# The SSD output projection as seven block products, the first norm's transposes later, and another split of the last output projection of cross attention

## The chip, the cores and the metric

The kernel runs on one core of one Trainium2 chip. The metric is device time in microseconds (us), the median of three runs. Engines: TensorE (PE) multiplies, VectorE (DVE) and ScalarE (ACT) work element by element, GpSimd (POOL) does a little of the same, SyncE (SP) issues most transfers.

## The reference

One post-norm decoder layer on 512 tokens of width 1024, everything in fp32. The kernel must give the layer's output for all 512 tokens.

```python
proj = x @ w_in                              # z, x|B|C, dt and q, k, v, gate
y_ssd = gated_rms_norm(ssd_scan(silu(conv(xbc)), dt) , silu(z))
y_ret = swish_gate(group_norm(retention(rotary(q), rotary(k), v)), g)
mix = concat(y_ssd, y_ret) @ w_out           # (512, 2048) @ (2048, 1024)
x = LN(ALPHA * x + mix)
k, v = mem @ w_xk, mem @ w_xv                # 256 memory tokens
x = LN(ALPHA * x + (softmax(x @ w_xq @ k.T * scale) @ v) @ w_xo)   # 4 heads of 256
x = LN(ALPHA * x + ffn(x))                   # up 1024 -> 2 x 2752, conv of 3, SiLU gate, down
```

## The kernel before

Every fp32 product is made of three fp32r matmuls (`mm3`): high part by high part, high by low, low by high. High parts are casts, low parts what the cast left. A weight group is 128 x 1024: `Group.split` loads it into one of three raw slots (L141, SyncE's queue), casts it on ScalarE (L143), and subtracts on VectorE (L144), or on GpSimd if the group was planned with `pool=True`. High and low part lie in a ring of four pairs `wh`, `wl`. `Stream` hands the groups out in the order of `plan`, loading ahead.

The 512 tokens are four tiles of 128 (`t` = 0 to 3). A product by tokens (`tok`) gives a PSUM bank of 128 tokens x 512 outputs, a product by features (`feat`) a bank of 128 features x tokens. Activations are split in the same way when they leave PSUM: ScalarE casts (L260), VectorE subtracts (L261).

For some projections the work is done in blocks: `Quarters` holds a weight as four quarters in two halves each and makes sums of quarters (L184 to L191); `Sides` does the same with the activations (splits L351 and L352, sums L372 to L375). Seven products of half the size in every direction, in the order 11, 21, T2, T1, T3, 22, T4, then replace eight; each is added into the accumulator `acc[t]` as it comes (L893, or L895 with the scale ALPHA). Their weight parts are made at L196 and L197. `SEVEN` lists the projections done so: the value projection `v` and the FFN's `down`. Between the products of `down`, groups of the up projection stand by the table `UP_MIX`.

TensorE's instructions are pinned in the order in which the program writes them; the other engines' order is set by a scheduler at build time from the dependencies. Each engine takes its queue strictly in order.

The stages that the change touches, in the order of the program:

- *Retention's output projection*, then the *SSD output projection*: eight weight groups, 24 matmuls of 128x512 each, for all four token tiles, and four additions at the end of each half (L893).
- *First norm*, beside the *memory keys*: `norm` takes the variance (L952, L953), a reciprocal root on GpSimd (L464, L465) and two scalings of 128x1024 (L957, L964). `norm_t` transposes the normed tile (eight transposes, L112). The keys are 8 features in 4 heads, 32 steps of six 128x256 matmuls; then 16 steps of the memory values. The low parts of the keys' eight weight groups are made on GpSimd. `first_norm` says after how many steps each tile's transposes come.
- *Cross attention*, four heads: `x_head(h)` weaves scores, softmax (maximum L1073, exponent L1076, reciprocal L1078, scaling L1080), transposes of the probabilities and values into dense work, which is the next head's query, and for the last head a part of the output projection `w_xo`.
- *Second norm*: `last` adds the rest of `w_xo` token by token (L1138), and each token is normed; the first up features follow, whose four low parts are made on GpSimd.
- *FFN*: up features with their convolution (L1173 on ScalarE, L1175 on VectorE) and the down products among them.

Of the kernel before, what the change touches and what calls it, by code (L numbers as in the profile page):

```python
# [9 lines left out]
F32R = mybir.dt.float32r  # L10
# [4 lines left out]
P = 128  # L15
T = 512
NT = 4
# [3 lines left out]
ALPHA = 2.0 ** 0.25  # L21
# [10 lines left out]
RAW = 3  # L32
NS = 37

SEVEN = ('v', 'down')
V_MIX = (1, 1, 1, 1, 0, 0, 0)
RET_MIX = (1, 1, 1, 1, 0, 0, 0)
UP_MIX = ((2, 2, 2, 2, 2, 2, 2), (1, 1, 1, 1, 1, 1, 1))

AHEAD = 4  # L40

# [18 lines left out]
def tile_layer(ctx, tc, wst, wdt, xt, xn, memt, rows, small_row, par, cst, mdec, out):  # L60
# [54 lines left out]
    def pair():  # L115
        return (ring.tile([P, 1024], F32R, tag="wh", name=nm("wh")),
                ring.tile([P, 1024], F32R, tag="wl", name=nm("wl")))
# [4 lines left out]
    class Group:  # L122
# [1 line left out]

        ahead = early = 0

        def __init__(self, n, pool=False):
            self.n, self.pool = n, pool

        def load(self):  # L130
            pass
# [3 lines left out]

        def split(self, parts=1, between=None):
            r = raw_slot()
            h, l = pair()
            for i in range(parts):
                c = slice(i * 1024 // parts, (i + 1) * 1024 // parts)  # L140
                nc.sync.dma_start(out=r[:, c], in_=wst[self.n][:, c])  # L141
                copy = nc.vector.tensor_copy if parts > 1 and i == 0 else nc.scalar.copy
                copy(out=h[:, c], in_=r[:, c])  # L143
                (gtt if self.pool else tt)(out=l[:, c], in0=r[:, c], in1=f(h[:, c]), op=sub)  # L144
                if between is not None:
                    between(i, copy)
            return h, l
# [72 lines left out]
            self.i += 1  # L220
            return h.rearrange("p (k f) -> p k f", k=n), l.rearrange("p (k f) -> p k f", k=n)

    def groups(n, k, pool=False):
        return [Group(n + i, pool) for i in range(k)]

    def mixed(products, others, after):

# [7 lines left out]
    plan = groups(0, 8)  # L235
# [1 line left out]
    plan += groups(28, 12)  # L237
    plan += mixed(Quarters(44).items(), groups(40, 4), RET_MIX) if "ret" in SEVEN else groups(40, 12)
    plan += [q for p in Quarters(52, 8, 3).items() for q in p] if "ssd" in SEVEN else groups(52, 8)
    plan += groups(60, 8, True) + groups(68, 24)  # L240
    plan += groups(92, 4, True)
    up, down = groups(96, 12) + groups(116, 16) + groups(140, 11), groups(151, 6)
    if "down" in SEVEN:
        plan += up[:14] + mixed(Quarters(108).items(), up[14:28], UP_MIX[0])
# [4 lines left out]
    W = Stream(plan)  # L249
# [5 lines left out]
    b = bank()  # L255
# [24 lines left out]
    def tok(lhs, ks, nt, done, first=False):  # L280
        bs = [bank() for _ in range(nt)]
        for kp in range(0, len(ks), 2):
            wh, wl = W.get(2)
            order = [(t, j) for t in range(nt) for j in range(2)]
            if first and kp == 0:
                order.sort(key=lambda o: o[1])
            for t, j in order:
                k = ks[kp + j]
                a = lhs(k, t)
                n = a[0].shape[0]  # L290
                mm3(bs[t], a, (wh[:n, j, :], wl[:n, j, :]), k == ks[0], k == ks[-1])
                if k == ks[-1]:
                    done(t, bs[t])
                if j:
                    yield
# [104 lines left out]
    def seq(*gens):  # L400
        for g in gens:
            yield from g
# [486 lines left out]
    def into_acc(n, scale=None):  # L889
        def done(t, b):  # L890
            a = acc[t][:, n * 512:(n + 1) * 512]
            if scale is None:
                tt(out=a, in0=a, in1=b, op=add)  # L893
            else:
                stt(out=a, in0=a, scalar=scale, in1=b, op0=mult, op1=add)  # L895
        return done
# [7 lines left out]
    def tok2(tiles):  # L904
        def lhs(k, t):
            return tiles[k][:, 0, t * P:(t + 1) * P], tiles[k][:, 1, t * P:(t + 1) * P]
        return lhs
# [127 lines left out]
    xT = new_x()  # L1035

    def first_norm():
        for t in range(NT):
            yield 8
            norm_t(t)  # L1040

    dense = seq(keys(), *[tok(m_lhs, all8, 2, v_mem(n)) for n in range(2)])
# [74 lines left out]
    for h in range(XH):  # L1117
        if h < XH - 1:
            dense = x_query(h + 1)
        else:  # L1120
            dense = seq(*[tok(tok2(OT), [0, 1, 2, 3], NT, into_acc(n, ALPHA)) for n in range(2)])
        weave(x_head(h), dense)
        drain(dense)


    def last(tiles, ks, t, gs, parts=HALVES):
        for part in parts:
            n, w = part.start // 512, part.stop - part.start
            c = slice(part.start % 512, part.start % 512 + w)
            b = bank()[:, :w]  # L1130
            for i in range(2):
                wh, wl = gs[2 * n + i]
                for j in range(2):
                    k = ks[2 * i + j]
                    a = tok2(tiles)(k, t)
                    p = a[0].shape[0]
                    mm3(b, a, (wh[:p, j, c], wl[:p, j, c]), i + j == 0, i + j == 2)
            tt(out=acc[t][:, part], in0=acc[t][:, part], in1=b, op=add)  # L1138
            yield

    gs = [W.get(2) for _ in range(4)]
    xT = new_x()
    for t in range(NT):
        ls = last(OT, [4, 5, 6, 7], t, gs)
        next(ls)
        if t == 3:
            norm_t(1)
        next(ls)
        norm(1, t)
        if t == 2:  # L1150
            norm_t(0)
# [148 lines left out]
def _pack(a):  # L1300
    import numpy as np
    f32 = np.float32
    a = {k: np.asarray(v) for k, v in a.items()}
    wi, wo = a["w_in"][0], a["w_mix_out"][0]
    up, dn = a["w_ffn_up"][0], a["w_ffn_down"][0]
    every = slice(None)
    g = []
    g.append(_tok(wi, every, slice(2576, 3600)))
    g.append((_quarters if "v" in SEVEN else _tok)(wi, every, slice(3600, 4624)))
    g.append(_feat(wi, slice(2048, 2560)))  # L1310
    g.append(_feat(wi, slice(1024, 2048)))
    g.append(_feat(wi, slice(4624, 5648)))
    g.append(_tok(wi, every, slice(0, 1024)))
    heads = np.concatenate([np.arange(P) + 1024 + P * h for h in (0, 2, 1, 3, 4, 6, 5, 7)])
    g.append(_quarters(wo, heads, every) if "ret" in SEVEN else _tok(wo, slice(1024, 2048), every))
    g.append((_quarters if "ssd" in SEVEN else _tok)(wo, slice(0, 1024), every))
    g.append(_feat(a["w_xk"][0], every))
    g.append(_tok(a["w_xv"][0], every, every))
    g.append(_feat(a["w_xq"][0], every))
    g.append(_tok(a["w_xo"][0], slice(0, 512), every))  # L1320
    g.append(_tok(a["w_xo"][0], slice(512, 1024), every))
    ug = []
    fcols = []
    for j in range(21):
        fcols.append(np.arange(P * j, P * j + P))
        fcols.append(np.arange(2752 + P * j, 2752 + P * j + P))
    fcols.append(np.concatenate([np.arange(2688, 2752), np.arange(5440, 5504)]))
    upg = _feat(up, np.concatenate(fcols))
    dnp = np.concatenate([dn, np.zeros((64, 1024), f32)], 0)
    down = _quarters if "down" in SEVEN else _tok  # L1330
    g.append(upg[0:16])
    g.append(down(dnp, slice(0, 1024), every))
    g.append(upg[16:32])
    g.append(down(dnp, slice(1024, 2048), every))
    g.append(upg[32:])
    g.append(_tok(dnp, slice(2048, 2304), every))
    g.append(_tok(dnp, slice(2304, 2816), every))
    wst = np.concatenate(g, 0)

    par = np.zeros((P, P_W), f32)  # L1340
    cw, cb = a["ssd_conv_w"][0], a["ssd_conv_b"][0]
    for i in range(12):
        for j in range(4):
            par[:, P_CONV + 5 * i + j] = cw[j, P * i:P * i + P]
        par[:, P_CONV + 5 * i + 4] = cb[P * i:P * i + P]
    par[:, P_GNW:P_GNW + 8] = a["ret_gn_w"][0].reshape(8, P).T
    par[:, P_GNB:P_GNB + 8] = a["ret_gn_b"][0].reshape(8, P).T
    fw = a["ffn_conv_w"][0]
    for i, cols in enumerate(fcols):
        for j in range(3):  # L1350
            par[:, P_FF + 5 * i + j] = fw[j, cols]
        par[:, P_FF + 5 * i + 3] = a["ffn_conv_b"][0][cols]
        par[:, P_FF + 5 * i + 4] = a["b_ffn_up"][0][cols]
    rows = np.concatenate([a[n] for n in ("ssd_norm_w", "ln1_g", "ln1_b", "ln2_g", "ln2_b", "ln3_g", "ln3_b")], 0)
    srow = np.concatenate([a[n] for n in ("ssd_dt_bias", "ssd_a_log", "ssd_d")], 1)
    x, mem = a["x"][0], a["mem"][0]
    cst, md = _consts()
    return {
        "wst": wst,
        "wdt": np.ascontiguousarray(wi[:, 2560:2576].reshape(KD, P, 16).transpose(1, 0, 2)).reshape(P, 128),  # L1360
        "xt": np.ascontiguousarray(x.T.reshape(4, 2, P, T).transpose(0, 2, 1, 3)).reshape(4, P, 1024),
        "xn": np.ascontiguousarray(x),
        "memt": np.ascontiguousarray(mem.T.reshape(2, 4, P, 256).transpose(0, 2, 1, 3)).reshape(2, P, 1024),
        "rows": rows,
        "srow": srow,
        "par": par,
        "cst": cst,
        "mdec": md,
    }
# [17 lines left out]
```

## Time and profile before

| | us |
|---|---|
| median of three runs (928.28 to 928.32) | 928.28 |
| the profiled execution | 928.88 |
| its span | 926.4 |
| TensorE busy, VectorE busy | 911.5 (98%), 648.4 (70%) |
| ScalarE busy, GpSimd busy | 369.6 (40%), 147.2 (16%) |
| span moved by DMA, mean | 103 GB/s |

The busy time of an engine is the time in which it executed something; where TensorE is busy, another engine's wait costs nothing. The granted clock of TensorE is 0.997 of full over the span. In the rows below, a line number is that of the kernel before.

### The profile page before, as it was taken

What the parts mean: (1) busy time and instruction counts of PE and PEld (TensorE: products, weight loads), DVE (VectorE), ACT (ScalarE), POOL (GpSimd) and SP (SyncE); (2) the same over time, 40 slices, a digit from 0 to 9 for tenths busy, and PEclk for the clock granted to TensorE, in tenths of its full rate; (3) what the DMA queues carried; (4) which work ended last, traced back from release to release, by engine and by line L of the source; (5) the groups of instructions that cost most, each with busy time, mean ns of one, the idle gap of its engine ahead of it and who ended that gap; (6) DMA issues with size and microseconds to landing.
All of it is one profiled execution on the core that took longest, in us unless ns stands there. A gap on an engine that the chain in (4) does not pass through costs nothing.

```text
span 926.4 us, 11580 instructions
## 1 busy us (share of the span) xinstructions
PE 911.5 (98%) x4535; PEld 757.0 (82%) x4535; DVE 648.4 (70%) x963; ACT 369.6 (40%) x545; POOL 147.2 (16%) x151
## 2 busy tenths in 40 slices
PE   9999999999999999999999999999999999999996
PEld 6788888877778888898888888988887888888885
DVE  5889757897854453478545669666779776897578
ACT  4236534355434431325434413543344443445330
POOL 1332011032525510163000007000000000000003
PEclk9999999999999999999999999999999999999998
DMA  7343122222212263426521222423333223331302
GB/s 287 105 146 127 39 76 69 69 69 70 69 46 69 91 230 109 138 92 205 190 82 46 69 69 95 134 91 98 108 133 118 68 69 114 125 119 52 114 23 91
DMA packets 26981, 95.24 MB, mean 103 GB/s; under 512 B 3120, under 2 KB 3632, under 8 KB 26928
## 3 DMA queue, kind: packets, MB, share of 16 engines
q1 hardware_dynamic: 25056, 88.09, 28.3%
q0 software_dynamic: 1728, 6.29, 2.0%
q8 instruction: 35, 0.57, 0.3%
q14 instruction: 18, 0.15, 0.0%
q10 hardware_dynamic: 144, 0.13, 0.0%
HBM read 92.41 MB, written 2.10 MB: 102 GB/s over the span
## 4 chain that ended last, share of the span: by engine, by line
PE 90%; DVE 5%; issue 1%; POOL 1%; DMA 1%; ACT 1%; SPq 0%; POOLq 0%; DVEq 0%
PE b L108 88%; PE b L112 3%; DVE s L964 1%; DMA s<-in_xt 1%; DVE s L957 1%; DVE st L952 1%; POOL st L465 1%; DVE s L1138 0%; DVE s L261 0%; DVE s L893 0%; DVE wl L197 0%; POOL st L464 0%; POOL s L960 0%; DVE wl L144 0%; DVE t L1175 0%
## 5 line engine op out<-in xcount | busy, mean ns | idle before, releaser
L108 PE MATMUL b<-s,wh 128*128 128x512 f32 (+1 forms) x1328 | 382.0, 372 | 3.3 <-DVE s L261 3.3
L108 PE MATMUL b<-wh,s 128*128 128x512 f32 (+1 forms) x1144 | 361.8, 391 | 0.6 <-DVE s L430 0.5
L108 PEld LDWEIGHTS b<-s,wh 128*128 128x128 f32 x1328 | 238.8, 189 | 47.2 <-DVE s L261 4.1
L108 PEld LDWEIGHTS b<-wh,s 128*128 128x128 f32 x1144 | 214.3, 188 | 48.3 <-DVE s L430 1.6
L144 DVE TENSOR_TENSOR wl<-raw,wh 128x1024 fp32r<-128x1024 f32 (+1 forms) x122 | 151.8, 1247 | 133.6 <-ACT wh L143 132.7
L108 PE MATMUL b<-s,wl 128*128 128x512 f32 (+1 forms) x664 | 245.1, 369 | 0.0
L143 ACT CAST wh<-raw 128x1024 fp32r<-128x1024 f32 (+1 forms) x133 | 139.2, 1049 | 215.8 <-PE b L108 195.1
L108 PE MATMUL b<-wl,s 128*128 128x512 f32 (+1 forms) x572 | 222.1, 388 | 1.4 <-DVE wl L197 1.4
L108 PEld LDWEIGHTS b<-s,wl 128*128 128x128 f32 x664 | 125.1, 188 | 21.3
L108 PEld LDWEIGHTS b<-wl,s 128*128 128x128 f32 x572 | 107.6, 188 | 23.6 <-DVE wl L197 1.7
L1175 DVE SCALAR_TENSOR_TENSOR t<-b,pr,t 128x511 f32<-128x511 f32 x86 | 64.2, 747 | 7.4 <-ACT t L1173 6.3
L197 DVE TENSOR_TENSOR wl<-s,wh 128x1024 fp32r<-128x1024 f32 x36 | 44.7, 1252 | 19.6 <-ACT wh L196 19.6
L196 ACT CAST wh<-s 128x1024 fp32r<-128x1024 f32 x36 | 37.8, 1053 | 50.2 <-PE b L108 40.7
L260 ACT CAST s<-b 128x512 fp32r<-128x512 f32 (+1 forms) x64 | 29.1, 484 | 55.7 <-PE b L112 22.5
L1201 POOL MEMSET t<- 64x512 f32 x1 | 0.5, 520 | 312.4 <-ACT t L1185 312.4
L144 POOL TENSOR_TENSOR wl<-raw,wh 128x1024 fp32r<-128x1024 f32 x12 | 32.7, 2738 | 68.2 <-ACT wh L143 68.2
L261 DVE TENSOR_TENSOR s<-b,s 128x512 fp32r<-128x512 f32 (+1 forms) x64 | 33.4, 550 | 13.9 <-ACT s L260 13.7
L1173 ACT ACTIVATE t<-b,cw,pr 128x512 f32<-128x512 f32 x43 | 33.3, 774 | 22.3 <-PE b L108 22.3
L893 DVE TENSOR_TENSOR s<-s,b 128x512 f32<-128x512 f32 x36 | 23.7, 680 | 15.4 <-PE b L108 15.4
L464 POOL TENSOR_TENSOR st<-st,epst 128x1 f32<-128x1 f32 (+1 forms) x16 | 5.6, 348 | 158.2 <-DVE st L953 157.8
L108 PEld LDWEIGHTS b<-s,t 128*128 128x128 f32 (+1 forms) x240 | 26.8, 180 | 3.1 <-PE b L108 0.9
L351 ACT CAST s<-s 128x512 fp32r<-128x512 f32 x36 | 20.7, 617 | 17.6 <-DVE s L1194 17.6
(164 smaller groups left out, 797.7 us busy)
## 6 DMA issues: line engine op xcount, KB each, us to landing
raw<-in_wst SPq DMA_DIRECT2D x132, 512.0 KB, 3.4
s<-in_wst SPq DMA_DIRECT2D x24, 512.0 KB, 4.7
s<-in_rows POOLq DMA_DIRECT2D x7, 512.0 KB, 6.2
s<-in_xn POOLq DMA_DIRECT2D x4, 512.0 KB, 5.8
s<-in_xt SPq DMA_DIRECT2D x3, 512.0 KB, 7.5
out_y<-s SPq DMA_DIRECT2D x3, 512.0 KB, 2.6
raw<-in_memt SPq DMA_DIRECT2D x2, 512.0 KB, 3.5
raw<-in_wst SPq DMA_DIRECT2D x2, 256.0 KB, 3.7
```

What stands on the lines that cost most here:

```text
L108: pin(nc.tensor.matmul(o, lhsT=lhsT, rhs=rhs, start=start, stop=stop, skip_group_check=more))
L112: pin(nc.tensor.transpose(o, i, ident[:p, :p]))
L143: copy(out=h[:, c], in_=r[:, c])
L144: (gtt if self.pool else tt)(out=l[:, c], in0=r[:, c], in1=f(h[:, c]), op=sub)
L196: nc.scalar.copy(out=h, in_=src)
L197: tt(out=l, in0=src, in1=f(h), op=sub)
L260: nc.scalar.copy(out=h, in_=src)
L261: tt(out=l, in0=src, in1=f(h), op=sub)
L351: nc.scalar.copy(out=h[:, c, :], in_=src)
L893: tt(out=a, in0=a, in1=b, op=add)
L1173: nc.scalar.activation(out=c, in_=u, func=AF.Identity, bias=cw[0][:, i:i + 1], scale=ffp[:, i, 2:3])
L1175: stt(out=c[:, d:], in0=u[:, :T - d], scalar=ffp[:, i, 2 - d:3 - d], in1=c[:, d:], op0=mult, op1=add)
```

## The change

The SSD output projection is made in seven products (`ssd` joins `SEVEN`): weights in `Quarters(52, 8, 3)`, which are loaded up to 8 groups ahead and whose sums are made up to 3 ahead, activations in `ssd_side`. Tokens 0 and 1 are normed after the sixth product, 2 and 3 after the seventh. The tables for `first_norm` and `UP_MIX` get other numbers. Of the output projection of cross attention, input tiles 0 and 1 (one head) are multiplied beside the last head, where 0 to 3 were, and the other six tiles token by token, where it was four; the weights of four of those groups have tiles of their own instead of ring pairs. The low parts of the first four up-feature groups are made on VectorE.

```diff
-SEVEN = ('v', 'down')
+SEVEN = ('v', 'ssd', 'down')
-UP_MIX = ((2, 2, 2, 2, 2, 2, 2), (1, 1, 1, 1, 1, 1, 1))
+UP_MIX = ((2, 3, 2, 2, 2, 2, 1), (1, 1, 1, 1, 1, 1, 1))
...
-            h, l = pair()
+            h, l = [big([P, 1024], F32R) for _ in range(2)] if self.own else pair()
...
-    plan += groups(60, 8, True) + groups(68, 24)
-    plan += groups(92, 4, True)
+    plan += groups(60, 8, True) + groups(68, 18) + groups(86, 4, own=True) + groups(90, 2)
+    plan += groups(92, 4)
...
     def first_norm():
-        for t in range(NT):
-            yield 8
+        for t, n in enumerate((13, 10, 10, 8)):
+            yield n
             norm_t(t)
...
-            dense = seq(*[tok(tok2(OT), [0, 1, 2, 3], NT, into_acc(n, ALPHA)) for n in range(2)])
+            dense = seq(*[tok(tok2(OT), [0, 1], NT, into_acc(n, ALPHA)) for n in range(2)])
...
-            for i in range(2):
-                wh, wl = gs[2 * n + i]
+            m = len(gs) // 2
+            for i in range(m):
+                wh, wl = gs[m * n + i]
...
-    gs = [W.get(2) for _ in range(4)]
+    gs = [W.get(2) for _ in range(6)]
...
-        ls = last(OT, [4, 5, 6, 7], t, gs)
+        ls = last(OT, [2, 3, 4, 5, 6, 7], t, gs)
```

VectorE's queue between the last retention groups and the first additions of the SSD projection. Before:

```order
L144 TENSOR_TENSOR wl_2887<-raw_2885,wh_2886 128x1024
L144 TENSOR_TENSOR wl_2917<-raw_2915,wh_2916 128x1024
L144 TENSOR_TENSOR wl_2947<-raw_2945,wh_2946 128x1024
L144 TENSOR_TENSOR wl_2977<-raw_2975,wh_2976 128x1024
L895 SCALAR_TENSOR_TENSOR s_2681<-s_2681,b_2881 128x512
L895 SCALAR_TENSOR_TENSOR s_2682<-s_2682,b_2882 128x512
L895 SCALAR_TENSOR_TENSOR s_2683<-s_2683,b_2883 128x512
L895 SCALAR_TENSOR_TENSOR s_2684<-s_2684,b_2884 128x512
```

And after the change, with the weight lows of the seven products (L197) and the sums of quarters (L184, L185, L189); `s_2681` to `s_2684` are the four accumulators:

```order
L144 TENSOR_TENSOR wl_2920<-raw_2918,wh_2919 128x1024
L197 TENSOR_TENSOR wl_2949<-s_2902,wh_2948 128x1024
L184 TENSOR_TENSOR s_2902<-s_2910,s_2902 128x1024
L185 TENSOR_TENSOR s_2976<-s_2912,s_2902 128x1024
L197 TENSOR_TENSOR wl_2980<-s_2904,wh_2979 128x1024
L189 TENSOR_TENSOR s_2910<-s_2912,s_2910 128x1024
L184 TENSOR_TENSOR s_2904<-s_2914,s_2904 128x1024
L185 TENSOR_TENSOR s_3007<-s_2916,s_2904 128x1024
L189 TENSOR_TENSOR s_2914<-s_2916,s_2914 128x1024
L197 TENSOR_TENSOR wl_3011<-s_2906,wh_3010 128x1024
```

What moved: sums of quarters, which wait for the quarters' transfers, stand ahead of the second and third weight lows.

GpSimd's queue beside the keys; `wl` are the low parts of the keys' weights, `st` the reciprocal roots of the four tokens (L464, L465). Before, from the first token's root on:

```order
L464 TENSOR_TENSOR st_3262<-st_3261,epst 128x1
L465 TENSOR_TENSOR st_3262<-st_3262,mhalf 128x1
L464 TENSOR_TENSOR st_3279<-st_3278,epst 128x1
L465 TENSOR_TENSOR st_3279<-st_3279,mhalf 128x1
L144 TENSOR_TENSOR wl_3336<-raw_3334,wh_3335 128x1024
L144 TENSOR_TENSOR wl_3366<-raw_3364,wh_3365 128x1024
L464 TENSOR_TENSOR st_3296<-st_3295,epst 128x1
L465 TENSOR_TENSOR st_3296<-st_3296,mhalf 128x1
L144 TENSOR_TENSOR wl_3418<-raw_3416,wh_3417 128x1024
L464 TENSOR_TENSOR st_3313<-st_3312,epst 128x1
L465 TENSOR_TENSOR st_3313<-st_3313,mhalf 128x1
L144 TENSOR_TENSOR wl_3448<-raw_3446,wh_3447 128x1024
```

And after the change, from the second weight group's low on:

```order
L144 TENSOR_TENSOR wl_3326<-raw_3324,wh_3325 128x1024
L464 TENSOR_TENSOR st_3316<-st_3315,epst 128x1
L465 TENSOR_TENSOR st_3316<-st_3316,mhalf 128x1
L144 TENSOR_TENSOR wl_3344<-raw_3342,wh_3343 128x1024
L144 TENSOR_TENSOR wl_3397<-raw_3395,wh_3396 128x1024
L464 TENSOR_TENSOR st_3357<-st_3356,epst 128x1
L465 TENSOR_TENSOR st_3357<-st_3357,mhalf 128x1
L144 TENSOR_TENSOR wl_3427<-raw_3425,wh_3426 128x1024
L144 TENSOR_TENSOR wl_3461<-raw_3459,wh_3460 128x1024
L464 TENSOR_TENSOR st_3374<-st_3373,epst 128x1
L465 TENSOR_TENSOR st_3374<-st_3374,mhalf 128x1
L144 TENSOR_TENSOR wl_3491<-raw_3489,wh_3490 128x1024
```

What moved: the roots stand further apart among the lows; the fifth low stands behind the third token's root, and the seventh behind the fourth's.

VectorE's queue in the last head's softmax, from the first maximum on (L1073; in the kernel after the change the lines behind L1130 are one lower). Before:

```order
L1073 TENSOR_REDUCE st_4394<-b_4381 128x2
L1074 TENSOR_SCALAR st_4395<-st_4394 128x2
L1073 TENSOR_REDUCE st_4417<-b_4404 128x2
L1078 RECIPROCAL st_4396<-st_4396 128x2
L1074 TENSOR_SCALAR st_4418<-st_4417 128x2
L1080 TENSOR_SCALAR t_773_4379<-t_773_4379,st_4396 128x256 x2
L1078 RECIPROCAL st_4419<-st_4419 128x2
L1080 TENSOR_SCALAR t_774_4380<-t_774_4380,st_4419 128x256 x2
```

And after the change:

```order
L1073 TENSOR_REDUCE st_4458<-b_4445 128x2
L144 TENSOR_TENSOR wl_4582<-raw_4580,wh_4581 128x1024
L1074 TENSOR_SCALAR st_4459<-st_4458 128x2
L1073 TENSOR_REDUCE st_4481<-b_4468 128x2
L895 SCALAR_TENSOR_TENSOR s_2684<-s_2684,b_4395 128x512
L1078 RECIPROCAL st_4460<-st_4460 128x2
L1074 TENSOR_SCALAR st_4482<-st_4481 128x2
L1080 TENSOR_SCALAR t_796_4443<-t_796_4443,st_4460 128x256 x2
L895 SCALAR_TENSOR_TENSOR s_2681<-s_2681,b_4498 128x512
L144 TENSOR_TENSOR wl_4588<-raw_4586,wh_4587 128x1024
L1078 RECIPROCAL st_4483<-st_4483 128x2
L895 SCALAR_TENSOR_TENSOR s_2682<-s_2682,b_4499 128x512
```

What moved: two weight lows (L144) and three additions of the output projection (L895) stand between the softmax's instructions, where there were none.

## Rows read from the trace of the kernel before

**Rows 1.** The page, section 1: busy time, share of the span, instructions of each engine.

```profile
PE 911.5 (98%) x4535; PEld 757.0 (82%) x4535; DVE 648.4 (70%) x963; ACT 369.6 (40%) x545; POOL 147.2 (16%) x151
```

**Rows 2.** Waits of TensorE: line waited for, us in total, times, longest.

```profile
PE b L108 <- DVE s L261: 3.3, 3, 1.7
PE b L108 <- DVE wl L197: 1.4, 1, 1.4
```

**Rows 3.** Windows: SSD out, then keys beside the norm; busy us and count of each engine.

```profile
core 0: us, PE busy (x) PEld busy (x) DVE busy (x) ACT busy (x) POOL busy (x), PEclk, DMA share, GB/s
360.10:403.40 43.30, 43.30 (x192) 35.85 (x192) 16.48 (x20) 10.34 (x10) 7.93 (x5) 1.00 0.36 114
403.40:424.00 20.60, 20.06 (x169) 19.79 (x167) 20.49 (x20) 6.33 (x9) 16.08 (x11) 1.00 0.30 97
```

**Rows 4.** VectorE lines, shapes apart: line, operation, names, shape, count, busy, mean ns, idle.

```profile
L197 DVE TENSOR_TENSOR wl<-s,wh 128x1024 fp32r<-128x1024 f32 x36 | 44.7, 1252 | 19.6 <-ACT wh L196 19.6
...
L893 DVE TENSOR_TENSOR s<-s,b 128x512 f32<-128x512 f32 x36 | 23.7, 680 | 15.4 <-PE b L108 15.4
...
L184 DVE TENSOR_TENSOR s<-s,s 128x1024 f32<-128x1024 f32 x6 | 7.3, 1223 | 0.1
```

**Rows 5.** Timeline of VectorE near the first retention products: start, duration.

```profile
333.11 1.22 DVE L144 TENSOR_TENSOR wl<-raw,wh 128x1024 fp32r<-128x1024 f32 x1 [2.38 <-ACT wh L143]
```

**Rows 6.** DMA in 320 to 400: GB/s in 40 slices of 2 us; landing of weights.

```profile
GB/s 205 57 174 401 385 406 279 391 303 20 41 229 0 117 145 0 205 57 6 256 0 43 219 0 150 121 0 254 244 51 242 262 78 184 0 20 242 0 72 199
...
raw<-in_wst SPq DMA_DIRECT2D x14, 512.0 KB, 3.4
```

**Rows 7.** Timeline of VectorE in the norm beside the keys.

```profile
404.10 1.28 DVE L964 SCALAR_TENSOR_TENSOR s<-s,st,s 128x1024 f32<-128x1024 f32 x1
405.30 3.43 DVE L957 SCALAR_TENSOR_TENSOR s<-s,st,s 128x1024 f32<-128x1024 f32 x1
...
420.48 3.42 DVE L964 SCALAR_TENSOR_TENSOR s<-s,st,s 128x1024 f32<-128x1024 f32 x1
```

**Rows 8.** Timeline of GpSimd in the same stretch.

```profile
399.33 2.40 POOL L144 TENSOR_TENSOR wl<-raw,wh 128x1024 fp32r<-128x1024 f32 x1 [3.05 <-ACT wh L143]
...
404.76 6.22 POOL L144 TENSOR_TENSOR wl<-raw,wh 128x1024 fp32r<-128x1024 f32 x2 [0.22 <-ACT wh L143]
...
418.90 1.54 POOL L465 TENSOR_TENSOR st<-st,mhalf 128x1 f32<-128x1 f32 x1
```

**Rows 9.** Timeline of TensorE in the keys: matmuls in pairs and single, transposes.

```profile
403.43 0.40 PE L108 MATMUL b<-s,wh 128*128 128x256 f32 x2
...
403.79 0.40 PE L108 MATMUL b<-s,wh 128*128 128x256 f32 x2
...
409.19 1.03 PE L112 MATMUL b<-cs,s 128*128 128x128 f32 x8
409.98 0.48 PE L108 MATMUL b<-s,wh 128*128 128x256 f32 x2
```

**Rows 10.** Timeline of VectorE in the last head's softmax.

```profile
523.91 0.69 DVE L1073 TENSOR_REDUCE st<-b 128x2 f32<-128x512 f32 x1 [0.54 <-PE b L108]
...
525.98 0.17 DVE L1078 RECIPROCAL st<-st 128x2 f32<-128x2 f32 x1 [0.62 <-ACT t L1076]
526.17 0.62 DVE L1080 TENSOR_SCALAR t<-t,st 128x256 f32<-128x256 f32 x2
```

**Rows 11.** Timeline of TensorE there: the transposes of the probabilities.

```profile
529.18 1.04 PE L112 MATMUL b<-cs,t 128*128 128x128 f32 x8
```

**Rows 12.** Timeline of TensorE at the first up features.

```profile
570.29 0.39 PE L108 MATMUL b<-s,wh 128*128 128x256 f32 x1 [1.37 <-DVE s L261]
...
571.54 0.39 PE L108 MATMUL b<-s,wh 128*128 128x256 f32 x1 [0.28 <-DVE s L261]
```

**Rows 13.** Timeline of TensorE at product T2 of the down projection.

```profile
708.96 0.50 PE L108 MATMUL b<-wl,s 128*128 128x512 f32 x1 [1.41 <-DVE wl L197]
```

**Rows 14.** The page, section 2: what the DMA queues moved over the span.

```profile
DMA packets 26981, 95.24 MB, mean 103 GB/s; under 512 B 3120, under 2 KB 3632, under 8 KB 26928
```

More of the change, by code (lines that the diff above doesn't have):

```diff
@@ L125, in tile_layer, with __init__ @@
         ahead = early = 0
-        def __init__(self, n, pool=False):
-            self.n, self.pool = n, pool
+        def __init__(self, n, pool=False, own=False):
+            self.n, self.pool, self.own = n, pool, own
         def load(self):
@@ L221, in get, with groups @@
             return h.rearrange("p (k f) -> p k f", k=n), l.rearrange("p (k f) -> p k f", k=n)
-    def groups(n, k, pool=False):
-        return [Group(n + i, pool) for i in range(k)]
+    def groups(n, k, pool=False, own=False):
+        return [Group(n + i, pool, own) for i in range(k)]
     def mixed(products, others, after):
@@ L1130, in last @@
             b = bank()[:, :w]
-            for i in range(2):
-                wh, wl = gs[2 * n + i]
+            m = len(gs) // 2
+            for i in range(m):
+                wh, wl = gs[m * n + i]
                 for j in range(2):
[L1134 to L1137, printed above, removed]
+                    a = tok2(tiles)(ks[2 * i + j], t)
+                    mm3(b, a, (wh[:, j, c], wl[:, j, c]), i + j == 0, i + j == m)
             tt(out=acc[t][:, part], in0=acc[t][:, part], in1=b, op=add)
             yield
-    gs = [W.get(2) for _ in range(4)]
+    gs = [W.get(2) for _ in range(6)]
     xT = new_x()
     for t in range(NT):
-        ls = last(OT, [4, 5, 6, 7], t, gs)
+        ls = last(OT, [2, 3, 4, 5, 6, 7], t, gs)
         next(ls)
@@ L1319, in _pack @@
     g.append(_feat(a["w_xq"][0], every))
-    g.append(_tok(a["w_xo"][0], slice(0, 512), every))
-    g.append(_tok(a["w_xo"][0], slice(512, 1024), every))
+    g.append(_tok(a["w_xo"][0], slice(0, 256), every))
+    g.append(_tok(a["w_xo"][0], slice(256, 1024), every))
     ug = []
```

## The prediction

> **What bounds the kernel now.** I read the busy times first: TensorE is busy 98% of the span, VectorE 70% [rows 1]. The reader is to see that only two things can move the time: fewer or cheaper matmuls, and the few gaps between them. The waits of TensorE show how small the gaps are: 3.3 us in three waits behind the low-part subtraction L261, 1.4 us in one wait for a weight low part L197 [rows 2]. Then I read the windows: in the SSD output projection (360.1 to 403.4) TensorE runs 43.30 us without a gap while VectorE has 16.48 us of work; in the next 20.6 us, memory keys beside the first norm, VectorE is busy 20.49 us and GpSimd 16.08 us [rows 3]. The first stage has room on VectorE, the second none. All durations are of the profiled execution (928.88 us, span 926.4, so 2.48 us around it); its 928.88 is 0.60 above the median 928.28, and I take the 0.60 off at the end.
>
> **SSD out as seven products.** 192 matmuls become 168. One costs 43.30/192 = 0.2255 us [rows 3]; 24 fewer are 5.4 us. What is added is VectorE work in this stage: 14 weight lows at 1.25 instead of 8 (three of the 14 belong to the stage before), two memory lows at the same size, sums at 1.22, 14 additions at 0.68 [rows 4] and the side parts, subtractions of the same shape. Issued back to back these start about 0.1 us closer than they last, so 15 big operations by 1.13 and 24 small ones by 0.6: about 31 us, with two norm statistics 33, inside 38 us of TensorE. With the releases in the printed order each weight low comes 4 us or more before its product. If that cover were gone, the excess of VectorE over 38 us would be the cost; the bounds are 0 and, if a third of the additions slipped into the weights' way, 3 us; I take 0, since TensorE's window shows how evenly the weights are asked for.
>
> The quarters (eight transfers of 0.52 MB, with two memory transfers ahead of them in SP's queue) cannot be issued before the slots' last readers are through, near the weight low that ends at 334.3 [rows 5]. The first weight sum must be done near 359, because VectorE's queue has it in front of the low part that the second retention product's successor needs. In the window 320 to 400 the queues moved 385 to 406 GB/s when several transfers stood in line [rows 6]; at 280, 4.7 MB need 17 us and are there by 351. Taken at 0.
>
> **The first norm beside the keys.** Here I follow the collision of VectorE and GpSimd. L964 takes 1.28 us alone; L957 right behind it takes 3.43, and the GpSimd lows beside it take 6.22 for two where one alone takes 2.40 [rows 7, 8]. 2 x 2.40 + 1.2 = 6.0: the two engines take turns, whole instruction by whole instruction. GpSimd's L465, which works on one column, took 1.54 at 418.90, while a scaling ran on VectorE [rows 8]. So a norm's scaling, the rsqrt and the lows w0 to w7 form one chain. In the kernel before, the gap of 1.7 us lay behind it (L261 queued behind the 3.42 us scaling at 420.48 [rows 7]: a PSUM bank came late for the last head).
>
> In the changed order tokens 0 and 1 are normed while the last product runs, and each rsqrt stands ahead of a low: w0, rsqrt 0, w1, rsqrt 1, w2, w3, rsqrt 2, w4, w5, rsqrt 3, w6, w7. Let K be the start of the keys (403.43 - 5.4 = 398.0). Token 0 is added up at K-6.6, token 1 at K-5.3. Taking turns (low 2.4, scaling 1.2): w0 by K-4.5, w1 K-0.4, second scaling of token 0 K+0.9, first of token 1 K+2.1, rsqrt 1 K+2.7, w2 K+5.1, scaling K+6.3, w3 K+8.7, first scaling of token 2 K+9.9, rsqrt 2 K+10.8, w4 K+13.2, scaling K+14.4, w5 K+16.8, scaling K+18.0, rsqrt 3 K+18.8, w6 K+21.2, scaling K+22.4, w7 K+24.8. TensorE needs them by its pace (three 128x256 matmuls in 0.36 us [rows 9], 24 of them 2.88 us a feature; eight transposes 0.79, from 409.19 to 409.98): w4 at K+12.4, w5 K+15.3, w6 K+19.0, w7 K+21.9. Each of the four is late by a little over what the one before it already cost: 0.8, 0.7, 0.7, 0.7, together 2.9 us. The old 1.7 goes, since the last head's bank now waits for an addition only. Net -1.2. Bounds: with no collisions +1.7; with two more turns lost, 5.3 us of waits, -3.6.
>
> [...]
>
> **Cross attention, last head.** The dense work between scores and probabilities is still four steps of 1.36 us, but VectorE's queue now holds, between the first maximum and the last scaling of probabilities, two weight lows (1.13 each) and three additions (0.6): 4.06 us that were not there. Before, it idled there 0.54 us ahead of the second maximum and 0.62 ahead of a reciprocal, and the last scaling ended near 527.4 (526.17 and two starts of 0.6) [rows 10]; so now 527.4 + 4.06 - 1.16 = 530.3. The transposes begin at 529.2 [rows 11], and, by the order, 0.1 us later in the new arrangement: a new wait of about 0.9. In exchange each token's later projection has 36 matmuls (8.1 us) instead of 24 for the same VectorE work, the four up-feature lows leave GpSimd, so that the second norm's L964 loses no turn to them, as the one at 420.48 did [rows 7], and the splits that released the gaps of 1.37 us at 570.29 and 0.28 us at 571.54 [rows 12] come about 1 us before they are needed. Matmuls here are as many as before. +1.65 - 0.9 = +0.75. Bounds: +1.65 with no new wait; if two of the weight casts in between wait 1.7 us more for their transfers (0.52 MB at the span's mean rate, 103 GB/s [rows 14], is 5.1 us, where the median landing is 3.4 [rows 6]), -2.6.
>
> **Up projection.** The 1.41 us wait at 708.96 is for product T2's second weight low [rows 13], queued behind sums and the convolution's L1175. One more feature (24 matmuls, 5.4 us) now stands between product 21 and T2. VectorE has this feature's convolution more in front (about 3 us), so the low is ready 16.7 us after product 21 and needed 19.0 after: the 1.41 goes. The feature taken from the end leaves the product after T4 one feature less, with no wait there before. +1.4; bounds 0 and 1.4.
>
> **Sum.** 5.4 - 1.2 + 0.75 + 1.4 = 6.35: 928.88 - 6.35 = 922.5, and less 0.60: **921.9**. After the down projection nothing changes.
>
> **Rivals.**
> *A, forecast:* as summed. Own range 920.4 to 923.4.
> *B, norms unhindered:* GpSimd wins the turns it needs, or the rsqrt slip in before a low; the keys give +1.0 to +1.7. Then 919.0 to 919.7. For it: the four lates are each under 1 us, and one swapped turn (w4 asks 0.4 us after the scaling) undoes them. Against: the turns of before went as my walk has them.
> *C, more waits:* the last head's casts wait for transfers (-2.6 for +0.75), or the norm loses two more turns (2 x 1.2). 924.3 to 925.3. For it: six weight groups now come in a row in the softmax; against: the weights' median landing is 3.4 us [rows 6].
> *D, slower:* the quarters come late. If they moved only at the span's mean of 103 GB/s, the eighth transfer in line (4.2 MB, 40.7 us) would land at 375.0 and VectorE's in-order queue would stop at the weight sum, so that the low behind it came near 379 where TensorE wants it at 362.8: 16 us late, 928.28 + 16 - 6.35 = 937.9. It decides slower once the delay is over 6.4 us, that is, below about 133 GB/s. Against it: the 385 to 406 GB/s above.
> *E, no change:* VectorE falls behind in the seven products by as much as they save; 928.3.
>
> **How the numbers follow.** A 0.51, B 0.20, C 0.16, D 0.07, E 0.06 (of which 0.05 within the 0.2%, 1.9 us, that a measurement here can tell, and 0.01 slower). Faster 0.87, same 0.05, slower 0.08. The range 918.5 to 925.8 holds A, nearly all of B and C; 921.9 is A's.
>
> **What would show it.** In the new profile: SSD out in about 38 us with no wait for L197 in it (D and E would show one); GpSimd's lows w4 to w7 each released late, waits of TensorE for L144 on GpSimd of about 0.7 us, four times, and none for L261 in the keys (B: none at all); one wait of about 0.9 us for L1080 before the last head's transposes (C: several us); no wait for L197 after T2. I am wrong if the SSD stage is not near 38 us, or if the sum of TensorE's gaps is under 2 or over 7 us.

## The result and the profile after

The changed kernel runs in 923.3 us, median of 4 runs (922.21 to 923.9), against 928.3 before: a ratio of 0.9939 (0.9925 to 0.9953). The forecast was 921.9. A second measurement gave 922.33 of 5 runs, ratio 0.993 (0.9916 to 0.9943). The profiled execution took 922.75 us with a span of 920.9, where before it was 928.88 and 926.4.

TensorE's waits in the new profile (line waited for, us in total, times, longest). What answers to [rows 2] is gone altogether, neither L261 nor L197 is there; two new waits stand in their place:

```profile
PE b L108 <- POOL wl L144: 1.9, 1, 1.9
...
PE b L108 <- ACT wh L143: 1.1, 1, 1.1
```

The windows over the SSD projection and the keys (columns as in [rows 3]):

```profile
core 0: us, PE busy (x) PEld busy (x) DVE busy (x) ACT busy (x) POOL busy (x), PEclk, DMA share, GB/s
359.50:397.65 38.15, 38.15 (x170) 31.59 (x169) 37.59 (x48) 19.97 (x24) 6.69 (x5) 1.00 0.12 42
397.65:425.00 27.35, 24.27 (x197) 23.53 (x196) 24.96 (x23) 8.89 (x14) 22.79 (x14) 1.00 0.35 118
```

TensorE has no gap in the SSD stage, though VectorE is busy 37.59 of 38.15 us where it had 16.48 of 43.30. The keys begin at 397.65 instead of 403.43. Against a mark common to both traces, TensorE's wait for L787 ahead of the stages that the change touches (254.35 before, 254.04 after), that is 149.08 and 143.61 us: 5.5 us saved. The gaps of [rows 12 and 13] are gone too. But behind the keys most of the first saving is given back: from the start of the keys to the last head's transposes of probabilities it is 125.75 us before (403.43 to 529.18 [rows 11]) and 129.40 after (397.65 to 527.05), 3.65 more. Here is where it went. GpSimd beside the keys, which answers to [rows 8]:

```profile
399.95 5.75 POOL L144 TENSOR_TENSOR wl<-raw,wh 128x1024 fp32r<-128x1024 f32 x2
...
407.43 5.74 POOL L144 TENSOR_TENSOR wl<-raw,wh 128x1024 fp32r<-128x1024 f32 x2
...
414.89 2.37 POOL L144 TENSOR_TENSOR wl<-raw,wh 128x1024 fp32r<-128x1024 f32 x1
421.29 2.36 POOL L144 TENSOR_TENSOR wl<-raw,wh 128x1024 fp32r<-128x1024 f32 x1 [4.03 <-ACT wh L143]
```

The lows w2 and w3 are the first row, w4 and w5 the second, then w6, and w7 last. 5.74 for two is 2 x 2.4 plus some 0.9 for a turn given up to VectorE. VectorE in the same stretch:

```profile
407.50 3.41 DVE L964 SCALAR_TENSOR_TENSOR s<-s,st,s 128x1024 f32<-128x1024 f32 x1
...
414.95 3.38 DVE L964 SCALAR_TENSOR_TENSOR s<-s,st,s 128x1024 f32<-128x1024 f32 x1
418.26 0.41 DVE L261 TENSOR_TENSOR s<-b,s 128x256 fp32r<-128x256 f32 x1
```

The scalings of 3.4 us are those beside a low, as in [rows 7]. ScalarE there, with what ended its idle time in brackets:

```profile
409.19 1.05 ACT L143 CAST wh<-raw 128x1024 fp32r<-128x1024 f32 x1 [2.09 <-DMA raw<-in_wst]
410.14 0.37 ACT L260 CAST s<-b 128x256 fp32r<-128x256 f32 x1
418.71 0.65 ACT L260 CAST s<-b 128x256 fp32r<-128x256 f32 x2 [8.20 <-DVE s L261]
...
420.17 1.05 ACT L143 CAST wh<-raw 128x1024 fp32r<-128x1024 f32 x1
```

Read it as a queue: the cast at 409.19 is w6's. At 410.14 the first quarter of token 0's transposes is cast; the next cast of the same bank waits 8.20 us for VectorE's split of the first (L261 at 418.26), which stands behind token 3's scaling of 414.95. Behind these casts in ScalarE's queue stands w7's, at 420.17, though the pair it needs had been free since the fourth feature's end near 410, and its transfer, issued at 409.85 when w4's low was done, had ended by 413 (from there on the DMA engines are idle for 1 us). The 8.20 us are one read of the bank waiting for another, ScalarE's for VectorE's, by the releaser in the row; what puts the two reads in order was not shown. So w7's low cannot begin before 421.29, and GpSimd, idle from 417.26, waits 4.03 us for it. On TensorE:

```profile
421.27 0.50 PE L108 MATMUL b<-s,wh 128*128 128x256 f32 x2 [1.06 <-ACT wh L143]
423.70 0.39 PE L108 MATMUL b<-s,wl 128*128 128x256 f32 x1 [1.93 <-POOL wl L144]
...
425.16 0.63 PE L108 MATMUL b<-s,wh 128*128 128x256 f32 x2
425.59 0.42 PE L108 MATMUL b<-s,wl 128*128 128x256 f32 x1
425.80 0.63 PE L108 MATMUL b<-s,wh 128*128 128x256 f32 x2
```

1.06 us for w7's high part and 1.93 for its low: 2.99 us in one place. The three rows at the end show something else: three 128x256 matmuls in 0.64 us (425.16 to 425.80), where they took 0.36 in [rows 9]. The windows give the granted clock (last column but two):

```profile
424.00:426.00 2.00, 2.00 (x14) 2.00 (x13) 1.82 (x4) 0.90 (x2) 0.71 (x2) 0.69 0.72 190
426.00:428.00 2.00, 2.00 (x11) 2.00 (x10) 1.55 (x3) 1.69 (x4) 0.00 (x0) 0.50 1.00 262
428.00:430.00 2.00, 2.00 (x13) 1.64 (x13) 1.79 (x3) 0.54 (x1) 0.00 (x0) 0.96 0.99 365
```

TensorE's granted clock falls to 0.50 for about 3.5 us behind the gap (0.51 in the mean from 424.70 to 428.20), with the engine busy all through (3.50 of 3.50 us). At 0.64 us for the work of 0.36, 3.5 us lose about 1.5. Gap 2.99 instead of 1.68, 1.5 of half clock, and 0.6 in small pauses before other lows make 3.4 of the 3.65; the rest is not assigned.

### The profile page after: what moved, and what is told of

The parts are those of the page before. It is cut to its first block, busy times and chain, and to the rows that moved or that the text cites. A ratio compares the mean times of both kernels' runs of the same rounds, so it can differ in the third digit from the quotient of the medians.

```text
span 920.9 us, 11604 instructions
## 1 busy us (share of the span) xinstructions
PE 907.6 (99%) x4511; PEld 753.9 (82%) x4511; DVE 679.9 (74%) x1001; ACT 383.1 (42%) x573; POOL 138.9 (15%) x147
## 4 chain that ended last, share of the span: by engine, by line
PE 92%; POOL 4%; DVE 2%; DMA 1%; ACT 1%; issue 1%; SPq 0%; POOLq 0%; DVEq 0%
PE b L108 89%; PE b L112 3%; POOL wl L144 2%; DMA s<-in_xt 1%; POOL st L464 1%; DVE s L964 0%; DVE st L952 0%; ACT wh L143 0%; POOL st L465 0%; POOL s L960 0%; DVE wl L144 0%; DVE s L1137 0%; DVE s L957 0%; DVE s L430 0%; SPq L141 0%
## 5 line engine op out<-in xcount | busy, mean ns | idle before, releaser
L108 PE MATMUL b<-wh,s 128*128 128x512 f32 (+1 forms) x1064 | 337.4, 391 | 0.5 <-DVE s L430 0.5
L108 PEld LDWEIGHTS b<-wh,s 128*128 128x128 f32 x1064 | 199.3, 188 | 44.8 <-DVE s L430 1.8
L144 DVE TENSOR_TENSOR wl<-raw,wh 128x1024 fp32r<-128x1024 f32 (+1 forms) x114 | 142.6, 1254 | 106.4 <-ACT wh L143 105.8
L108 PE MATMUL b<-wl,s 128*128 128x512 f32 (+1 forms) x532 | 206.4, 388 | 0.0
L196 ACT CAST wh<-s 128x1024 fp32r<-128x1024 f32 x50 | 52.6, 1053 | 78.2 <-PE b L108 58.3
L197 DVE TENSOR_TENSOR wl<-s,wh 128x1024 fp32r<-128x1024 f32 x50 | 61.6, 1241 | 21.3 <-ACT wh L196 21.3
L260 ACT CAST s<-b 128x256 fp32r<-128x256 f32 (+1 forms) x56 | 24.9, 465 | 61.5 <-PE b L112 27.9
L108 PE MATMUL b<-s,s 128*128 128x512 f32 (+2 forms) x232 | 48.8, 360 | 0.0
L108 PEld LDWEIGHTS b<-s,s 128*128 128x128 f32 x232 | 36.6, 190 | 7.4 <-issue 2.9
L261 DVE TENSOR_TENSOR s<-b,s 128x256 fp32r<-128x256 f32 (+1 forms) x56 | 28.7, 532 | 13.3 <-ACT s L260 13.0
L352 DVE TENSOR_TENSOR s<-s,s 128x512 fp32r<-128x512 f32 x50 | 33.5, 695 | 3.0 <-ACT s L351 3.0
L144 POOL TENSOR_TENSOR wl<-raw,wh 128x1024 fp32r<-128x1024 f32 x8 | 21.8, 2735 | 68.6 <-ACT wh L143 68.6
```

The source lines that it names most:

```text
L108: pin(nc.tensor.matmul(o, lhsT=lhsT, rhs=rhs, start=start, stop=stop, skip_group_check=more))
L196: nc.scalar.copy(out=h, in_=src)
L197: tt(out=l, in0=src, in1=f(h), op=sub)
L260: nc.scalar.copy(out=h, in_=src)
L261: tt(out=l, in0=src, in1=f(h), op=sub)
L352: tt(out=l[:, c, :], in0=src, in1=f(h[:, c, :]), op=sub)
```

## The experiments

Theory S: each saving stands by itself; what the keys give back is one gap, since w7's cast stands in ScalarE's queue behind casts that wait for VectorE, and the half clock behind the gap. Rivals: R, it comes from the later transposes and not from the seven products; P, it is GpSimd and VectorE taking turns that makes the last low late, wherever its cast stands; G, the half clock has nothing to do with the gap.

**One part alone, and all but one.** The first kernel is the one before with `SEVEN = ('v', 'ssd', 'down')` alone, the second the changed one with

```diff
-SEVEN = ('v', 'ssd', 'down')
+SEVEN = ('v', 'down')
```

> The kernel before with the SSD projection in seven products alone (transposes of the norm after 8 steps each, old split of the cross attention's projection, old up mix). Theory S (each saving stands by itself, and the keys pay a gap in which the last low is late, with a lower clock behind it): 5.4 us off in the SSD stage, the gaps of 1.65 us at the first up features and of 1.4 us at T2 stay, the keys' gap 2 to 4 us with up to 1.8 us of lower clock: 925 to 927. Rival R (the seven products cost nothing in the keys, and the loss comes from the later transposes): 923.0 to 923.5.

> The kernel after with the SSD projection in eight weight groups again, everything else kept. S: 5.4 us more in the SSD stage, the gaps at the first up features and at T2 stay away (3.1 us), the keys without a fall of the clock: 923.5 to 925.5. R: the keys' gap is still there, as the later transposes make it: 926 to 928.

Measured: 924.14 us, ratio 0.9957 (0.9942 to 0.9972), and 923.25 us, 0.9952 (0.9937 to 0.9966); the kernel before stood at 927.76 on that chip. The first saves 3.6 us, less than the 5.4 of its matmuls. Its gap in the keys is the old one, a bank behind a split:

```profile
419.68 0.50 PE L108 MATMUL b<-s,wh 128*128 128x256 f32 x2 [1.94 <-DVE s L261]
```

and behind it the clock is low:

```profile
420.00:424.00 4.00, 4.00 (x23) 4.00 (x22) 3.33 (x7) 4.00 (x9) 3.32 (x3) 0.57 0.01 2
```

The second has no such thing; its only wait in the keys is

```profile
424.95 0.39 PE L108 MATMUL b<-s,wl 128*128 128x256 f32 x1 [0.42 <-POOL wl L144]
```

so the three smaller edits are worth about 4.5 us without the seven products. Added up, 3.6 and 4.5 are 8.1 us, where the changed kernel saves 5.0 to 6.0: the parts collide in the keys. Neither forecast of the first was met, S was nearly met by the second, and R, as far as it makes the later transposes harmful by themselves, falls with it. Of the first kernel's four runs one took 922.21 us at a mean granted clock of 0.998, the others 924.01 to 924.55 at 0.996: the half clock seems to be missing in that one, but only one of the four was profiled.

**The transposes' places.** The table of `first_norm` in the changed kernel, set back and set later:

```diff
-        for t, n in enumerate((13, 10, 10, 8)):
+        for t, n in enumerate((8, 8, 8, 8)):
...
+        for t, n in enumerate((22, 9, 6, 6)):
```

> The kernel after with the norm's transposes after 8 steps each again. S: the last low's cast on ScalarE still stands behind splits of token 0's transposes, and those behind VectorE's scaling; the gap stays within 1 us of the 3.0 us in the changed kernel: 922 to 925. R: the gap goes: 918.5 to 920.

> The kernel after with the norm's transposes after 22, 9, 6 and 6 steps, so that ScalarE's cast of the keys' last weight group stands ahead of the casts of token 0's transposes. S: the cast no longer waits, the low is made right behind the one before it; the gap falls from 3.0 us to 1 us or less and the clock stays up: 918 to 920.5. Rival P (GpSimd and VectorE taking turns are what makes the last low late, wherever its cast stands): the gap stays above 2 us: 922 to 924.

Measured: 919.5 us, ratio 0.9909 (0.9893 to 0.9926), and 918.63, 0.9902 (0.9887 to 0.9917). With 8 steps the gap is not gone, but it is the old one for the bank, and the clock stays up:

```profile
419.25 0.51 PE L108 MATMUL b<-s,wh 128*128 128x256 f32 x2 [1.92 <-DVE s L261]
```

```profile
419.20:421.00 1.80, 1.75 (x14) 1.75 (x15) 1.21 (x3) 1.80 (x5) 0.75 (x1) 1.00 0.24 96
```

S had the gap stay near 3 us there; it is 1.92. So beside seven products the new table costs 0.003 of the time (2.8 us) against the old one: in this R is right, and the loss takes both, the seven products and the later transposes. What R had wrong is that the gap would go. With the old table w7's cast is late too (419.11), and its low with it:

```profile
420.25 2.42 POOL L144 TENSOR_TENSOR wl<-raw,wh 128x1024 fp32r<-128x1024 f32 x1 [3.33 <-ACT wh L143]
```

But TensorE, held up one feature earlier by the bank, comes to w7 only near 422. With 22 steps ScalarE casts w7 at 412.19, as soon as its transfer is there. That is ahead of token 0's casts, whose wait of 2.86 us for VectorE comes after, and GpSimd makes w6 and w7 in one go:

```profile
412.19 1.06 ACT L143 CAST wh<-raw 128x1024 fp32r<-128x1024 f32 x1 [2.99 <-DMA raw<-in_wst]
...
417.97 0.36 ACT L260 CAST s<-b 128x256 fp32r<-128x256 f32 x1
421.19 0.65 ACT L260 CAST s<-b 128x256 fp32r<-128x256 f32 x2 [2.86 <-DVE s L261]
```

```profile
414.00 5.74 POOL L144 TENSOR_TENSOR wl<-raw,wh 128x1024 fp32r<-128x1024 f32 x2
```

What is left for TensorE at w7 is

```profile
419.80 0.39 PE L108 MATMUL b<-s,wl 128*128 128x256 f32 x1 [0.21 <-POOL wl L144]
```

and the same twice, 0.32 and 0.21, at w4 and w5. The turns of GpSimd and VectorE are all still there (two lows in 5.74 us as before); P falls, the cast's place was it. No other kernel tried was faster.

**Side by side.** The base of the next runs is the kernel with 22, 9, 6 and 6 steps; with it on one chip, the changed kernel again, and the base with one part undone each:

```diff
-            dense = seq(*[tok(tok2(OT), [0, 1], NT, into_acc(n, ALPHA)) for n in range(2)])
+            dense = seq(*[tok(tok2(OT), [0, 1, 2, 3], NT, into_acc(n, ALPHA)) for n in range(2)])
...
-UP_MIX = ((2, 3, 2, 2, 2, 2, 1), (1, 1, 1, 1, 1, 1, 1))
+UP_MIX = ((2, 2, 2, 2, 2, 2, 2), (1, 1, 1, 1, 1, 1, 1))
```

> The kernel with the norm's transposes after 22, 9, 6 and 6 steps once more, as the base of the others of this group and to be set against the changed kernel on the same chip. S: 918 to 919.2, TensorE's gaps in the keys under 1 us and no stretch at half clock there.

> The changed kernel itself on the same chip. S: 3.7 to 5.5 us above the base (3.0 us gap less 0.7, and 1.5 to 3 us of half clock behind the gap): 922 to 924. Rival P: under 2.5 us above the base, since the gap alone is 2.3 more.

> The base with the old split of the cross attention's output projection (four tiles beside the last head, four token by token); the low parts of the first up features stay on VectorE. S: the gap at the first up features comes back, 1 to 1.7 us: 919.6 to 920.8. Rival L (taking the lows off GpSimd was enough, since it was GpSimd that held up the scaling): no gap there, 918 to 919.2.

> The base with the old table of up features among the down products. S: the wait for T2's second weight low comes back, 1.4 us: 919.6 to 920.8, and nothing else moves. Rival: other features behind T2 catch up the wait, 918.3 to 919.2.

Measured, with 928.36 before: base 919.33, ratio 0.9899 (0.9886 to 0.9913); changed kernel 922.33, 0.993 (0.9916 to 0.9943); old split 923.14, 0.9937 (0.9925 to 0.995); old table 920.86, 0.9916 (0.9902 to 0.9929). The changed kernel is 3.0 us above the base, between the two forecasts. In its profiled run the mean granted clock is low again, 0.995 against 0.999 in the base's. The first stage adds noise: the base's profiled run reached the wait for L787 at 254.29, the other at 253.30. Counted from that mark to the end of the span, the changed kernel takes 666.9 us (666.8 in the first profile), the base 663.2 (and 663.2 in its first), so 3.7, the lower end of S. With the old split the gap at the first up features is 2.45 us though GpSimd has no low there:

```profile
565.58 0.38 PE L108 MATMUL b<-s,wh 128*128 128x256 f32 x1 [2.45 <-DVE s L261]
...
566.84 0.58 PE L108 MATMUL b<-s,wh 128*128 128x256 f32 x1 [0.29 <-DVE s L261]
```

so L falls. But the gap is not quite the old one: three weight lows on VectorE (L144, 1.21 us each, at 559.26, 561.59 and 563.05) now stand among the splits, where before the change a scaling took 3.42 us beside GpSimd's lows. It cost 3.8 us, more than S said; the clock was 0.83 and 0.75 in the 8 us from 564 on. With the old table the wait for T2 is back to the hundredth, and nothing else:

```profile
701.74 0.50 PE L108 MATMUL b<-wl,s 128*128 128x512 f32 x1 [1.41 <-DVE wl L197]
```

**The gap by itself.** In the base, the low of group 67, the keys' last, is written two and three times:

```diff
-                (gtt if self.pool else tt)(out=l[:, c], in0=r[:, c], in1=f(h[:, c]), op=sub)
+                for _ in range(2 if self.n == 67 else 1):
+                    (gtt if self.pool else tt)(out=l[:, c], in0=r[:, c], in1=f(h[:, c]), op=sub)
```

> The base (transposes after 22, 9, 6, 6) with the low part of the keys' last weight group written twice on GpSimd, the second time with the same values: TensorE waits 2.4 us more at the same place in the keys where the changed kernel has its 3.0 us, with no other instruction moved. Theory C (a gap of this size brings TensorE's clock to half for some us behind it): gap 2.6 us, then a stretch at half clock that costs 1.5 to 2 us: 4 to 4.5 us above the base, 923 to 924. Rival G (the clock falls in the changed kernel for another reason, such as the transfers or the collisions around it): gap only, 2.4 us above the base, 921.5 to 922.

> The same low written three times: gap 5 us. C: half clock behind it for as long as after the shorter gap or longer, 6.5 to 8 us above the base: 925.5 to 927.5. G: 4.8 us above the base: 924 to 924.5.

Measured: 924.06 us, ratio 0.996 (0.9945 to 0.9975), and 927.56, 0.9991 (0.9982 to 1.0001). The gaps are longer than said: a repeated low adds 3.3 us and not the 2.4 of one alone; the other 0.9, as in the 5.74 us for two, goes by estimate to turns given up to VectorE. Twice:

```profile
423.29 0.58 PE L108 MATMUL b<-s,wl 128*128 128x256 f32 x1 [3.50 <-POOL wl L145]
```

```profile
422.00:425.00 3.00, 1.71 (x8) 1.71 (x9) 2.54 (x5) 1.75 (x4) 2.31 (x3) 0.70 0.24 57
425.00:428.00 3.00, 3.00 (x21) 3.00 (x21) 0.39 (x2) 1.22 (x3) 0.00 (x0) 0.73 1.02 296
```

Three times:

```profile
427.76 0.58 PE L108 MATMUL b<-s,wl 128*128 128x256 f32 x1 [6.79 <-POOL wl L145]
```

```profile
424.00:427.00 3.00, 0.00 (x0) 0.00 (x0) 2.24 (x3) 0.93 (x3) 2.92 (x2) 0.74 0.00 0
427.00:430.00 3.00, 2.23 (x10) 2.24 (x11) 0.00 (x0) 0.00 (x0) 1.78 (x3) 0.50 0.44 139
```

Against the base's 0.99 of the time they cost 0.006 and 0.009, 5.6 and 8.4 us (4.8 and 8.7 counted from the mark); the gaps grew by 3.3 and 6.6. The rest, 1.5 to 2.3 us each, is the half clock: G falls, since nothing but that low was changed. In the longer gap the clock fell while TensorE stood idle, and it still was at 0.50 when the matmuls came back.

**What GpSimd does.** In the base the up features' first lows go back to GpSimd (`groups(92, 4, True)`); in the changed kernel the keys' lows go to VectorE (`groups(60, 8)`):

> The base with the low parts of the first four up-feature groups on GpSimd again, the new split of the cross attention's projection kept. S: the norm's scalings take turns with the lows again (3.4 us each beside a low), but the longer work per token covers that: no gap at the first up features over 0.5 us, 919 to 919.8. Rival L: the gap comes back, 1.4 us or more: 920.4 to 922.

> The changed kernel (transposes after 13, 10, 10, 8) with the low parts of the keys' weights on VectorE instead of GpSimd. S: no scaling over 1.4 us, since GpSimd has no long instruction beside it; but the fourth group's low stands in VectorE's queue behind token 2's scalings, so a gap of 1.5 to 3 us comes up there instead, with or without a fall of the clock: 920.5 to 923. Rival P (the turns with GpSimd are all that fails): no gap in the keys, 918.3 to 919.5.

Measured: 918.65 us, ratio 0.9902 (0.9887 to 0.9917), and 919.6, 0.991 (0.9895 to 0.9924). The first is the base's time, just under S's range; there is no gap at the up features, so with the new split the lows can be on either engine. VectorE in the second norm:

```profile
564.15 1.57 DVE L957 SCALAR_TENSOR_TENSOR s<-s,st,s 128x1024 f32<-128x1024 f32 x1
568.78 1.29 DVE L964 SCALAR_TENSOR_TENSOR s<-s,st,s 128x1024 f32<-128x1024 f32 x1 [3.06 <-POOL st L465]
```

No scaling lost a turn of 3.4 us: the lows on GpSimd began at 562.23, behind two of the norms, and what they delayed was token 2's root (3.06 us of waiting), which the longer work per token covers. The second kernel has scalings of 1.27 us throughout and a gap where S had it, at the fourth low behind token 2's scalings:

```profile
405.29 1.27 DVE L964 SCALAR_TENSOR_TENSOR s<-s,st,s 128x1024 f32<-128x1024 f32 x1
...
406.59 1.17 DVE L144 TENSOR_TENSOR wl<-raw,wh 128x1024 fp32r<-128x1024 f32 x1
```

```profile
407.82 0.38 PE L108 MATMUL b<-s,wl 128*128 128x256 f32 x1 [2.19 <-DVE wl L144]
```

Its clock was 0.57 from 408 to 412. It is 2.7 us faster than the changed kernel all the same (some 1.4 counted from the mark, in the profiled runs), and outside S's time by 0.9 us. Here too the runs differ: 920.15 and 920.09 us at mean clocks of 0.995 and 0.996, 919.12 and 918.83 at 0.998 and 0.997.

## Why the prediction was right, point by point

- *SSD out.* 5.4 forecast, 5.5 measured on the common mark, no wait for L197 in the stage. D and E did not come: the quarters were there. It was closer than forecast: VectorE was to need 33 of 38 us and was busy 37.59 of 38.15, most of token 0's two scalings (1.27 and 2.76 us) among it. Two slips of the working change nothing: eight quarters and two memory transfers are 5.2 MB and not 4.7, there by 353 at 280 GB/s, and D turns slower below about 136 GB/s, not 133.
- *The first norm beside the keys.* The step that was mis-sized: -1.2 forecast, -3.65 measured. The turns went as walked, only 1.3 to 1.6 us earlier: w5 done at K+15.5, w6 at K+19.6 (K = 397.65), where the walk had 16.8 and 21.2. So w4 to w6 cost at most the 0.6 us of small pauses and not 2.2. w7 was done at K+26.0 and not 24.8, and for another reason: the walk followed VectorE and GpSimd and left out ScalarE, whose cast of w7 stood behind casts that waited for VectorE. That the gaps' sum (2.99 and 0.6) came out near the 2.9 forecast is an accident of these two errors. What the sum had no term for at all is the half clock, about 1.5 us.
- *Cross attention.* +0.75 forecast, about +1.4 measured. The forecast misread a row: the one at 526.17 in [rows 10] holds both scalings (`x2`, 0.62 us in all), so before the change the last ended at 526.79 and not near 527.4. From there its working comes out: 526.79 + 4.06 - 1.16 = 529.69. Measured is 527.54 (526.93 and 0.61), which is 529.67 on the old axis (2.13 later, as the transposes begin at 527.05 and 529.18):

```profile
525.13 1.22 DVE L144 TENSOR_TENSOR wl<-raw,wh 128x1024 fp32r<-128x1024 f32 x1
...
526.93 0.61 DVE L1080 TENSOR_SCALAR t<-t,st 128x256 f32<-128x256 f32 x2
```

```profile
527.05 1.31 PE L112 MATMUL b<-cs,t 128*128 128x128 f32 x8
528.12 0.48 PE L108 MATMUL b<-wh,s 128*128 128x512 f32 x1
```

  So the last scaling ended 0.49 us behind the transposes' start, and the eight transposes ended 0.28 us late (1.07 from start to the next matmul, where 0.79 is usual), since the first of them need the other token pair, whose scalings were done. The forecast had 0.9 (1.0 by its own ends, 530.3 and 529.3), of which 0.6 is the misread row. The gaps of 1.65 are gone: +1.4. That the up features' lows left GpSimd was not needed for it, as the run with these lows back on GpSimd shows. VectorE's scaling there is undisturbed, and the splits come in time:

```profile
560.89 1.28 DVE L964 SCALAR_TENSOR_TENSOR s<-s,st,s 128x1024 f32<-128x1024 f32 x1
...
563.02 1.08 DVE L261 TENSOR_TENSOR s<-b,s 128x256 fp32r<-128x256 f32 x3
```

- *Up projection.* +1.4 forecast; the wait of 1.41 is gone, and back with the old table.
- *Sum.* 5.5 - 3.65 + 1.4 + 1.4 = 4.65; the span is 5.5 shorter, 0.3 of it in the first stage. The other 0.5 lies behind the transposes; most of it may be the up projection, since undoing its table cost 1.8 us counted from the mark and not 1.41. The 923.3 lies 1.4 above the forecast, about the half clock, and just inside A's own range (to 923.4). That it lies there is in part luck: the keys came out 2.45 us worse than their term, cross attention and what is not assigned about 1.2 better. Of the rivals C's time came closest, by none of its reasons; B, with norms that nothing hinders, did not come.

## What to carry to other kernels

When a change makes one engine's work denser, walk every queue between it and the engine that bounds, not only the two that contend: an in-order ScalarE queue passed VectorE's delay (8.20 us at one cast) on to a weight that had nothing to do with it. Set work whose input is late behind the work that others wait for: the order of w7's cast and token 0's casts was worth 3.0 to 3.7 us, at no cost. Count a gap on TensorE with what its clock does behind it (0.50 for about 3.5 us behind 2.99 here, some 1.5 us lost). And read what a row with `x2` holds before building on its end.

## What the runs showed of the hardware that was not expected

The granted clock of TensorE fell behind gaps of 1.94 us (SSD alone, 0.57 in the mean of 420 to 424), 2.19 (keys' lows on VectorE, 0.57 in 408 to 412), 2.45 (old split, 0.60 in 566 to 569), 2.99 (0.50 in 426 to 428), 3.50 (0.73 in 425 to 428) and 6.79 us (0.50 in 427 to 430). Where it was worked out (2.99, 3.50 and 6.79) it cost about 1.5 to 2.3 us each time: at 0.50 three 128x256 matmuls took 0.64 us for 0.36, which is less than double. Behind the gaps of 1.41 us and 1.68 us (before) it did not fall (1.00 in 709 to 714 and 425 to 430), nor in the profiled run with 1.92 us (1.00 in 419.2 to 427). 1.92 without and 1.94 with are too near each other for the length of the gap alone to decide, and runs of one kernel seem to differ in it (922.21 us at a mean clock of 0.998 against 924.01 to 924.55 at 0.996 with the SSD projection alone); what decides was not tried. One GpSimd subtraction of 128x1024 and one VectorE scaling of the same size did not slow each other by a share: where they met, their times fit turns, one behind the other, as in [rows 7 and 8]. In the changed kernel the first of two lows, begun at 407.43, would be done at 409.83 with the 2.40 of one alone; the scaling begun at 407.50 ended 1.08 us behind that, at 410.91 (1.27 alone), and the second low 2.26 behind the scaling, at 413.17. What makes them take turns was not shown.
